# Operand addresses of a TensorE-bound layer moved to 52 bytes apart, with two small moves of work around it

## The chip, the cores and the metric

The kernel runs on one core of a Trainium2 chip, as one program. The metric is the device time of one execution in microseconds. A TensorE matmul is two instructions here: a load of the stationary operand (128 columns), and a matmul that streams the moving operand past it. The load for the next matmul runs beside the current matmul, so both read SBUF at the same time.

## The reference

One decoder layer on x of 512 tokens by 2048 features, all in float32:

```python
xn = rmsnorm(x, norm_w)
proj = xn @ w_in                         # 2048 -> 14352 columns
q, k, v, o, z, i, f, u_g, v_g, z_g = split(proj)
# group A: causal conv + SiLU on q, k; 8 mLSTM heads (chunks of 128, gates from i, f);
#          per-head RMSNorm, then * sigmoid(o) * silu(z)
# group B: gelu(u_g) * (tril(w_spatial) @ layernorm(gelu(v_g)) + b_spatial) * silu(z_g)
y = concat(y_m, y_g)                     # 4096
out = rmsnorm(x + y @ w_out, final_norm_w)
```

## The kernel before

**Products in three passes.** A float32 operand is split into a rounded part (`wh`, `xah`, ...: a cast by ACT to float32r) and a rest (`wl`, `xal`, ...: a subtraction by DVE), and each product is three matmuls: high with high, high with low, low with high.

**Phase A, the input projection**, is 28 units (`unit_order`), each with 8 chunks of the contraction. Unit 0 is computed directly: four PSUM banks `p_0` to `p_3` (one for each 128 tokens), matmuls with 512 moving columns (L760 to L769; the gate columns, L282, run beside it). Units 1 to 27 use a scheme of seven products for a 2x2 block (`PRODUCTS`, the function `products`, L798): a chunk is 7 products x 2 halves x 3 passes = 42 matmuls with 256 moving columns, into seven banks, which `combine` (L371 to L378) adds up on DVE at the unit's end. That is 27 x 8 x 42 = 9,072 matmuls. In a token unit the stationary operand is a slice of x and the moving one a slice of w; in the four `qk` units (features) it is the other way round. A chunk of weights comes by a DMA from SP (L150) with an adding DMA from POOL (L151) on top, and is split by `split` (L183 to L187): `wf` is the raw chunk, `we` two sums made by DVE, `wh` and `wl` the split tiles of 7 x 256 columns.

**Phase B, the output projection**, has 32 chunks of kind `g` (direct, 512 columns, L853 to L855), beside which the mLSTM heads are computed, 24 chunks of kind `m` (seven products again, the same L798: 1,008 matmuls), and a last part in 512 columns (L917 to L919).

**What sets the order.** Everything that follows a unit (activations, norms, transposes, the heads) is put on a queue `bg`, of which the loops take a few items after each chunk (`run_bg(3)` in phase A, `run_bg(6)` in phase B). The code's order is only a priority: when the program is built, a scheduler puts each engine's instructions into one fixed queue, by that priority and by when it takes operands and buffers to be ready. Tiles of one tag share a fixed number of buffers, handed out in the code's order (12 for `temp`).

**At the end of unit 0** ACT reads the four banks with a GELU (L774) into the tiles `e_00` to `e_11`; `bn_stats` on DVE (L411) follows, from `after_vv`. Products q1, q6, q2 and q7 of unit 1 need the banks of `p_0`, `p_1`, `p_2` and `p_3` in that order. **At the end of unit 27** a loop (L815) empties `bg`: the sigmoid and SiLU of the last unit (L496, `after_oz`) come before phase B's own work.

**Where operands lie.** The pools are laid out one after the other, with two gaps (`GAP_X`, `GAP_W`) and an offset inside the direct chunks' tiles (`OFF`). In the built program the start addresses are, in bytes modulo 128: x operands and the seven-product w tiles 0 and 64, so that moving and stationary operands of L798 start 64 apart; operands of the 512-column matmuls 0 and 0, but for the `a21` tiles (`a` in the profile; stationary in a fourth of unit 0's matmuls) at 32.

Of the kernel before, what the change touches and what calls it, by code (L numbers as in the profile page):

```python
# [9 lines left out]
F32 = mybir.dt.float32  # L10
# [22 lines left out]
    ("q1", 0, 1), ("q6", 4, 5), ("q2", 1, 0), ("q7", 3, 4), ("q5", 6, 3), ("q4", 2, 6), ("q3", 5, 2),  # L33
]
WS = 7 * H
OFF = 16
GAP_X, GAP_W = 24, 112


def unit_order():  # L40
# [7 lines left out]
def hybrid_layer(ctx, tc, xs, x, w_first, w_mid, w_gate, w_out, w_last, par, bif, ws_t, sgu, fin_w, out):  # L48
# [17 lines left out]
    def temp(name, dt=F32):  # L66
        return tp.tile([P, S], dt, tag="t", name=name)
# [11 lines left out]
    for w in range(9):  # L79
# [16 lines left out]
    mask = one.tile([P, P], F32, name="mask")
    nc.gpsimd.memset(mask, 0.0)
    nc.gpsimd.affine_select(
        out=mask, in_=mask, pattern=[[1, P]], compare_op=ALU.is_ge,
        fill=BIG, base=0, channel_multiplier=-1,  # L100
    )
# [17 lines left out]
    chunks = []  # L119
    for un in range(NA):  # L120
        for j in range(NP):
            chunks.append(("std", w_first[j]) if un == 0 else ("str", w_mid[un - 1, j]))
    NB0 = len(chunks)
    b_chunks = []
    for kind in "gm":
# [26 lines left out]

    def split_first(a):
        if 0 not in splits:
            splits[0] = tuple(wp.tile([P, WS], F32R, tag=tag, name=f"{tag}0", bufs=3)[:, OFF:OFF + 1024].rearrange(
                "p (a b) -> p a b", a=2) for tag in ("wh", "wl"))
        h, l = splits[0]
        f = raws[0][:, a * S:(a + 1) * S]
        nc.scalar.copy(h[:, a, :], f)
        nc.vector.tensor_tensor(l[:, a, :], f, h[:, a, :].bitcast(F32), op=ALU.subtract)  # L160

    def split(n):
        if n >= NCH or n in splits:
            return
        kind = chunks[n][0]
        t = raws[n]
        raws[n] = None
        if kind == "std":
            if n >= NF0 + 2:
                h = xb.tile([P, 2, S], F32R, tag="xb", name=f"fh{n}")  # L170
                l = xb.tile([P, 2, S], F32R, tag="xb", name=f"fl{n}")
            else:
                h, l = (wp.tile([P, WS], F32R, tag=tag, name=f"{tag}{n}", bufs=bufs)[
                    :, OFF:OFF + 1024].rearrange("p (a b) -> p a b", a=2) for tag, bufs in (("wh", 3), ("wl", 3)))
            f = t[:, 0:1024].rearrange("p (a b) -> p a b", a=2)
            nc.scalar.copy(h, f)  # L176
            nc.vector.tensor_tensor(l, f, h.bitcast(F32), op=ALU.subtract)  # L177
            splits[n] = (h, l)
            return
        h = wp.tile([P, WS], F32R, tag="wh", name=f"wh{n}", bufs=3)  # L180
        l = wp.tile([P, WS], F32R, tag="wl", name=f"wl{n}", bufs=3)
        e = wp.tile([P, 2 * H], F32, tag="we", name=f"we{n}", bufs=1)
        nc.vector.tensor_tensor(e[:, 0:H], t[:, 3 * H:4 * H], t[:, 2 * H:3 * H], op=ALU.add)  # L183
        nc.vector.tensor_tensor(e[:, H:2 * H], e[:, 0:H], t[:, 0:H], op=ALU.add)  # L184
        for f, c in ((t, slice(0, 5 * H)), (e, slice(5 * H, WS))):
            nc.scalar.copy(h[:, c], f)  # L186
            nc.vector.tensor_tensor(l[:, c], f, h[:, c].bitcast(F32), op=ALU.subtract)  # L187
        splits[n] = tuple(v.rearrange("p (a b) -> p a b", a=7) for v in (h, l))
# [58 lines left out]
            nc.scalar.activation(t, t, AF.Square, accum_out=ssq8[:, tt, c:c + 1])  # L247

    def stats_end():
        ssq = sm.tile([P, NT], F32, tag="s4", name="ssq", bufs=8)  # L250
        nc.vector.reduce_sum(ssq, ssq8, axis=mybir.AxisListType.X)
        nc.vector.tensor_scalar(ssq, ssq, 1.0 / D, EPS, op0=ALU.mult, op1=ALU.add)
        nc.gpsimd.tensor_tensor(r_tok, ssq, mhalf[:, :NT], op=ALU.pow)
# [143 lines left out]
    def after_vv(i, c):  # L397
        mv = sm.tile([P, 2, NT, 2], F32, tag="mv", name=f"mv{i}")
        rs = sm.tile([P, 2, NT], F32, tag="rs", name=f"rs{i}")
        nm = sm.tile([P, 2, NT], F32, tag="nm", name=f"nm{i}")  # L400
        for g in range(2):
            vn[2 * i + g] = [c[0][g], c[1][g]]

        def gelu(g, a):
            for t in range(2):
                tt = 2 * a + t
                d = c[a][g][:, t, :]
                if i > 0:
                    nc.scalar.activation(d, d, AF.Gelu_apprx_tanh, scale=r_tok[:, tt:tt + 1])
                st = sm.tile([P, 6], F32, tag="st", name=f"st{i}_{tt}_{g}", bufs=4)  # L410
                nc.vector.bn_stats(st, d)  # L411
                nc.vector.bn_aggr(mv[:, g, tt, :], st)

        def scales():
            vv = sm.tile([P, 2, NT], F32, tag="vv", name=f"vv{i}")
            nc.vector.tensor_scalar(vv, mv[:, :, :, 1], EPS, None, op0=ALU.add)
            nc.gpsimd.tensor_tensor(rs, vv, mhalf.rearrange("p (a b) -> p a b", a=2), op=ALU.pow)
            nc.vector.scalar_tensor_tensor(nm, in0=mv[:, :, :, 0], scalar=-1.0, in1=rs, op0=ALU.mult, op1=ALU.mult)

        def norm(g, a):  # L420
            d = c[a][g]
            for t in range(2):
                tt = 2 * a + t
                nc.scalar.activation(d[:, t, :], d[:, t, :], AF.Identity, scale=rs[:, g, tt:tt + 1],
                                     bias=nm[:, g, tt:tt + 1])
            wb = wb_t[2 * i + g]
            nc.vector.tensor_tensor(d, d, wb[:, 0:1, :].to_broadcast([P, 2, H]), op=ALU.mult)
            nc.vector.tensor_tensor(d, d, wb[:, 1:2, :].to_broadcast([P, 2, H]), op=ALU.add)

        bg.append(lambda: st_ws(i))  # L430
        for g in range(2):
            for a in range(2):
# [112 lines left out]
    def st_load_v(h):  # L545
        for a in range(2):
            t = half(f"vr{h}_{a}")
            nc.gpsimd.dma_start(t, v_dram[h][:, 2 * a:2 * a + 2, :])
            hi, lo = (xa.tile([P, 3 * H], F32R, tag="xa", name=f"v{c}{h}_{a}").rearrange(
                "p (a b) -> p a b", a=2)[:, :, 112:370] for c in "hl")  # L550
            for t2, one_or_zero in ((hi, 1.0), (lo, 0.0)):
                nc.gpsimd.memset(t2[:, :, H:258].bitcast(F32), one_or_zero)
            nc.scalar.copy(hi[:, :, 0:H], t)
            nc.vector.tensor_tensor(lo[:, :, 0:H], t, hi[:, :, 0:H].bitcast(F32), op=ALU.subtract)
            v_t[h].append((hi, lo))
# [5 lines left out]
    def st_s(h, s0):  # L561
# [9 lines left out]
        pt = temp(f"p{h}_{s0}")  # L571
        cb = cb_t[h]
        g = gst[:, pair(s0, s0), h:h + 1]
        nc.vector.scalar_tensor_tensor(pt[:, 0:P], in0=cb[:, s0 * P:(s0 + 1) * P], scalar=g, in1=mask,
                                       op0=ALU.subtract, op1=ALU.max)
        nc.scalar.activation(pt[:, 0:P], pt[:, 0:P], AF.Exp, scale=-1.0)
        for t0 in range(s0 + 1, NT):
# [34 lines left out]
    def st_norm(h):  # L612
# [3 lines left out]
            nc.gpsimd.dma_start(t, oz_dram[h][:, 2 * a:2 * a + 2, :])  # L616
            oz_t[h].append(t)
        ht = h_t[h]
        da = sm.tile([P, NT], F32, tag="s4", name=f"da{h}", bufs=8)
        nc.vector.scalar_tensor_tensor(da, in0=den_t[h], scalar=-1.0, in1=den_t[h], op0=ALU.mult, op1=ALU.max)  # L620
        nc.vector.tensor_tensor(da, da, gst[:, 10:14, h], op=ALU.max)
        rr = sm.tile([P, NT], F32, tag="s4", name=f"rr{h}", bufs=8)
        nc.vector.reciprocal(rr, da)
        ssq = sm.tile([P, NT], F32, tag="s4", name=f"sq{h}", bufs=8)
        junk = temp(f"jk{h}")[:, 0:H]
        for t0 in range(NT):
            nc.scalar.activation(junk, ht[t0 // 2][:, t0 % 2, 0:H], AF.Square, scale=rr[:, t0:t0 + 1],
                                 accum_out=ssq[:, t0:t0 + 1])
        nc.vector.tensor_scalar(ssq, ssq, 1.0 / H, EPS, op0=ALU.mult, op1=ALU.add)
        rn = sm.tile([P, NT], F32, tag="s4", name=f"rn{h}", bufs=8)  # L630
        nc.gpsimd.tensor_tensor(rn, ssq, mhalf[:, :NT], op=ALU.pow)
        hc = sm.tile([P, NT], F32, tag="hc", name=f"hc{h}", bufs=4)
        nc.vector.tensor_tensor(hc, rr, rn, op=ALU.mult)
# [78 lines left out]
    def run_bg(k):  # L712
        while k > 0 and bg:
            bg.popleft()()
            k -= 1
# [2 lines left out]
        while tag not in done:  # L718
            bg.popleft()()

    act_warm = sm.tile([P, 8], F32, tag="aw", name="act_warm", bufs=1)
    nc.scalar.copy(act_warm, mhalf)

    load_x(0)
# [46 lines left out]
    c0 = [[half(f"e0_{a}{g}") for g in range(2)] for a in range(2)]  # L771
    for q in range(4):
        for g in range(2):
            nc.scalar.activation(c0[q // 2][g][:, q % 2, :], acc[q][:, g * H:(g + 1) * H], AF.Gelu_apprx_tanh,  # L774
                                 scale=r_tok[:, q:q + 1])
# [25 lines left out]
    for un in range(1, NA):  # L801
        kind, i = order[un]
        q = product_banks(un)
        for j in range(NP):
# [7 lines left out]
            if un == NA - 1 and j >= 1:  # L812
                load_y("g", j - 1)
            run_bg(3)
    while bg:  # L815
        run_bg(1)
    load_y("g", NP - 1)
    bg.append(gates)
    queue_loads(0)
    bg.extend([pause] * 6)  # L820
    bg.append(gate_shifts)
# [200 lines left out]
```

## Time and profile before

| | us |
|---|---|
| median of 3 runs (1563.46, 1564.47, 1569.3) | 1564.47 |
| the profiled execution, its own time | 1571.57 |
| span of the profiled execution | 1569.9 |
| TensorE (PE) matmul busy / load busy (PEld) | 1545.9 / 1485.4 |
| DVE busy / ACT busy / POOL busy | 1183.7 / 874.6 / 285.3 |

A busy PE says only that some matmul is under way: a matmul of 256 columns is recorded as 0.28 us long, while the next starts some 0.12 us after it, so that two or three overlap. How fast PE goes is read from the starts: from a pair of rows of the timeline, or from how many matmuls fall into a stretch of given length.

### The profile page before, as it was taken

What the parts mean: (1) busy time and instruction counts of PE and PEld (TensorE: products, weight loads), DVE (VectorE), ACT (ScalarE), POOL (GpSimd) and SP (SyncE); (2) the same over time, 40 slices, a digit from 0 to 9 for tenths busy, and PEclk for the clock granted to TensorE, in tenths of its full rate; (3) what the DMA queues carried; (4) which work ended last, traced back from release to release, by engine and by line L of the source; (5) the groups of instructions that cost most, each with busy time, mean ns of one, the idle gap of its engine ahead of it and who ended that gap; (6) DMA issues with size and microseconds to landing.
All of it is one profiled execution on the core that took longest, in us unless ns stands there. A gap on an engine that the chain in (4) does not pass through costs nothing. (4 is left out here: it accounts for less than half of the span.)

```text
span 1569.9 us, 30095 instructions
## 1 busy us (share of the span) xinstructions
PE 1545.9 (98%) x11864; PEld 1485.4 (95%) x11864; DVE 1183.7 (75%) x1944; ACT 874.6 (56%) x1340; POOL 285.3 (18%) x384
## 2 busy tenths in 40 slices
PE   9999999999999999999999999999999999999997
PEld 7899999999999999999999999999988788889986
DVE  8787767877966876976877977678887665697875
ACT  6665455654654555554655565454776666553333
POOL 1411112211122211121211111111202222011100
PEclk9999999999999999999999999999999999999999
DMA  9777878787788777778787777877964665798962
GB/s 319 210 192 187 228 177 209 185 202 193 213 203 215 188 211 184 210 190 214 192 211 186 200 203 199 212 201 196 277 195 156 206 226 188 238 265 238 277 231 107
DMA packets 118510, 326.99 MB, mean 208 GB/s; under 512 B 13534, under 2 KB 20702, under 8 KB 118369
## 3 DMA queue, kind: packets, MB, share of 16 engines
q1 hardware_dynamic: 77456, 243.30, 48.1%
q0 software_dynamic: 40192, 80.66, 26.7%
q8 instruction: 93, 1.52, 0.4%
q10 hardware_dynamic: 720, 1.11, 0.2%
q14 instruction: 49, 0.39, 0.1%
HBM read 229.37 MB, written 32.74 MB: 167 GB/s over the span
## 5 line engine op out<-in xcount | busy, mean ns | idle before, releaser
L186 ACT CAST wh<-wf 128x1280 fp32r<-128x1280 f32 x240 | 301.9, 1264 | 379.9 <-issue 237.8
L187 DVE TENSOR_TENSOR wl<-wf,wh 128x1280 fp32r<-128x1280 f32 x240 | 356.7, 1488 | 174.3 <-ACT wh L186 174.0
L798 PE MATMUL q<-wh,xbh 128*128 128x256 f32 x1472 | 413.7, 281 | 1.4 <-ACT e L774 1.4
L798 PE MATMUL q<-wl,xbh 128*128 128x256 f32 x1472 | 412.9, 281 | 1.2 <-DVE wl L187 1.2
L798 PE MATMUL q<-wh,xbl 128*128 128x256 f32 x1472 | 412.7, 280 | 0.0
L151 POOL DMA_DIRECT2D wf<-wf x240 | 205.3, 857 | 1010.9 <-DMA wf<-w_mid 243.2
L798 PE MATMUL q<-wh,xah 128*128 128x256 f32 x1104 | 311.8, 282 | 0.0
L798 PE MATMUL q<-wl,xah 128*128 128x256 f32 x1104 | 309.5, 280 | 0.0
L798 PE MATMUL q<-wh,xal 128*128 128x256 f32 x1104 | 309.4, 280 | 0.0
L798 PEld LDWEIGHTS q<-wh,xbh 128*128 128x128 f32 x1472 | 281.1, 191 | 1.8 <-ACT e L774 1.6
L798 PEld LDWEIGHTS q<-wl,xbh 128*128 128x128 f32 x1472 | 276.9, 188 | 1.9 <-DVE wl L187 1.8
L798 PEld LDWEIGHTS q<-wh,xbl 128*128 128x128 f32 x1472 | 276.3, 188 | 0.0
L798 PEld LDWEIGHTS q<-wh,xah 128*128 128x128 f32 x1104 | 210.8, 191 | 0.7 <-ACT e L774 0.2
L798 PEld LDWEIGHTS q<-wl,xah 128*128 128x128 f32 x1104 | 207.7, 188 | 0.1
L798 PEld LDWEIGHTS q<-wh,xal 128*128 128x128 f32 x1104 | 207.2, 188 | 0.0
L186 ACT CAST wh<-we 128x512 fp32r<-128x512 f32 x240 | 148.2, 618 | 89.6 <-DVE we L184 89.2
L187 DVE TENSOR_TENSOR wl<-we,wh 128x512 fp32r<-128x512 f32 x240 | 164.7, 686 | 17.2 <-ACT wh L186 17.2
L183 DVE TENSOR_TENSOR we<-wf 128x256 f32<-128x256 f32 x240 | 101.4, 422 | 20.0 <-issue 9.0
L184 DVE TENSOR_TENSOR we<-we,wf 128x256 f32<-128x256 f32 x240 | 101.4, 423 | 5.4
L853 PE MATMUL og<-wh,ygh 128*128 128x512 f32 x256 | 100.9, 396 | 1.6 <-ACT wh L176 1.6
L854 PE MATMUL og<-wl,ygh 128*128 128x512 f32 x256 | 101.5, 397 | 0.1
L855 PE MATMUL og<-wh,ygl 128*128 128x512 f32 x256 | 101.3, 396 | 0.0
(284 smaller groups left out, 2865.9 us busy)
## 6 DMA issues: line engine op xcount, KB each, us to landing
wf<-w_mid SPq DMA_DIRECT2D x216, 640.0 KB, 4.7
wf<-wf POOLq DMA_DIRECT2D x240, 256.0 KB, 5.2
wf<-w_out_p SPq DMA_DIRECT2D x40, 512.0 KB, 4.1
wf<-w_last SPq DMA_DIRECT2D x24, 640.0 KB, 5.7
xr<-xs SPq DMA_DIRECT2D x16, 256.0 KB, 6.1
xt<-x SPq DMA_DIRECT2D x8, 512.0 KB, 7.5
ozd<-e SPq DMA_DIRECT2D x16, 256.0 KB, 2.6
ygd<-yfg SPq DMA_DIRECT2D x16, 256.0 KB, 4.5
```

The lines of the kernel that those rows point to most:

```text
L151: nc.gpsimd.dma_start(t[:, 3 * H:5 * H], t[:, H:3 * H], accum_op=ALU.add)
L183: nc.vector.tensor_tensor(e[:, 0:H], t[:, 3 * H:4 * H], t[:, 2 * H:3 * H], op=ALU.add)
L184: nc.vector.tensor_tensor(e[:, H:2 * H], e[:, 0:H], t[:, 0:H], op=ALU.add)
L186: nc.scalar.copy(h[:, c], f)
L187: nc.vector.tensor_tensor(l[:, c], f, h[:, c].bitcast(F32), op=ALU.subtract)
L798: nc.tensor.matmul(o, lhsT=st_, rhs=mv_, start=(first and a == 0), stop=(last and a == 2), skip_group_check=True)
L853: nc.tensor.matmul(acc[q], lhsT=yh[:, kk, cs], rhs=wh[:, kk, :], start=st, stop=False)
L854: nc.tensor.matmul(acc[q], lhsT=yh[:, kk, cs], rhs=wl[:, kk, :], start=False, stop=False)
L855: nc.tensor.matmul(acc[q], lhsT=yl[:, kk, cs], rhs=wh[:, kk, :], start=False, stop=sp_)
```

## The change

It does three things.

1. The split tiles of the seven-product chunks start at other places. Their slots grow by 64 columns (`WSLOT`), and a chunk lies 3 columns into it (`OFF_TOK`) for a token unit and for phase B, 29 columns (`OFF_FEAT`) for a `qk` unit; the gaps shrink, and the v operands of the heads move from column 112 to 115. In the built program the moving operand of L798 then starts at 76 and the stationary one at 0 modulo 128 bytes (`qk` units: 0 and 52): the stationary operand is 52 bytes beyond the moving one in both. The 512-column operands stay at 0 and 0, `a21` goes from 32 to 64. To make room, `mask` and `act_warm` become `temp` tiles (the mask is made by POOL after phase A) and the tag `s4` has 6 buffers in place of 8.
2. At the end of unit 0 the banks are emptied as scaled copies, `p_0` and `p_2` by ACT, `p_1` and `p_3` by DVE; the GELU runs afterwards, in SBUF, as an item of `bg`.
3. The loop that empties `bg` before phase B is gone: what is left of unit 27 is taken by phase B's `run_bg(6)`.

```diff
-OFF = 16
-GAP_X, GAP_W = 24, 112
+WSLOT = WS + 64
+OFF, OFF_TOK, OFF_FEAT = 16, 3, 29
+GAP_X, GAP_W = 16, 48
...
-            chunks.append(("std", w_first[j]) if un == 0 else ("str", w_mid[un - 1, j]))
+            chunks.append(("std", w_first[j]) if un == 0 else
+                          ("strf" if order[un][0] == "qk" else "str", w_mid[un - 1, j]))
...
-        h = wp.tile([P, WS], F32R, tag="wh", name=f"wh{n}", bufs=3)
-        l = wp.tile([P, WS], F32R, tag="wl", name=f"wl{n}", bufs=3)
+        o = OFF_FEAT if kind == "strf" else OFF_TOK
+        h, l = (wp.tile([P, WSLOT], F32R, tag=tag, name=f"{tag}{n}", bufs=3)[:, o:o + WS] for tag in ("wh", "wl"))
...
-                if i > 0:
-                    nc.scalar.activation(d, d, AF.Gelu_apprx_tanh, scale=r_tok[:, tt:tt + 1])
+                nc.scalar.activation(d, d, AF.Gelu_apprx_tanh, scale=r_tok[:, tt:tt + 1] if i > 0 else 1.0)
...
-                "p (a b) -> p a b", a=2)[:, :, 112:370] for c in "hl")
+                "p (a b) -> p a b", a=2)[:, :, 115:373] for c in "hl")
...
-    act_warm = sm.tile([P, 8], F32, tag="aw", name="act_warm", bufs=1)
+    act_warm = temp("act_warm")[:, 0:8]
...
-            nc.scalar.activation(c0[q // 2][g][:, q % 2, :], acc[q][:, g * H:(g + 1) * H], AF.Gelu_apprx_tanh,
-                                 scale=r_tok[:, q:q + 1])
+            d, ps = c0[q // 2][g][:, q % 2, :], acc[q][:, g * H:(g + 1) * H]
+            if q % 2:
+                nc.vector.tensor_scalar(d, ps, r_tok[:, q:q + 1], None, op0=ALU.mult)
+            else:
+                nc.scalar.activation(d, ps, AF.Copy, scale=r_tok[:, q:q + 1])
...
-    while bg:
-        run_bg(1)
     load_y("g", NP - 1)
     bg.append(gates)
+    bg.append(make_mask)
```

The scheduler moves instructions with it, at three places. First, the start. `act_warm` is a scratch copy that waits for a memset on POOL; `a_0` is the high part of the `a21` tile. ACT before:

```order
L217 CAST xah_186<-xr_172 128x256
L218 CAST a_0_188<-xr_172 128x256
L159 CAST wh_193<-wf_174 128x512 x2
L223 CAST xah_186<-xr_172 128x512
L217 CAST xah_208<-xr_178 128x256
L218 CAST a_1_210<-xr_178 128x256
L722 COPY act_warm<-mhalf 128x8
```

ACT with the change, at the same place:

```order
L224 CAST xah_181<-xr_167 128x256
L166 CAST wh_188<-wf_169 128x512 x2
L230 CAST xah_181<-xr_167 128x512
L224 CAST xah_203<-xr_173 128x256
L230 CAST xah_203<-xr_173 128x512
L728 COPY act_warm<-mhalf 128x8
L225 CAST a_0_183<-xr_167 128x256
```

`a_0` now comes after `act_warm`, whose tile is handed out before it; PE does the twelve matmuls of `p_0` and `p_1` first and those of `p_2` and `p_3`, which need `a_0`, after them. Second, the end of unit 0. DVE with the change (`e_..` are the copies, `st` and `mv` the statistics, `we` and `wl` the next chunk's split):

```order
L417 BN_STATS st_0_0_829<-e_00_734 128x6
L190 TENSOR_TENSOR we_675<-wf_609 128x256
L782 TENSOR_SCALAR e_00_734<-p_1_218,r_tok 128x256
L191 TENSOR_TENSOR we_675<-we_675,wf_609 128x256
L782 TENSOR_SCALAR e_01_735<-p_1_218,r_tok 128x256
L418 BN_AGGR mv_749<-st_0_0_829 128x2
L417 BN_STATS st_1_0_833<-e_00_734 128x6
L418 BN_AGGR mv_749<-st_1_0_833 128x2
L417 BN_STATS st_2_0_891<-e_10_736 128x6
L782 TENSOR_SCALAR e_10_736<-p_3_220,r_tok 128x256
```

DVE's copies of `p_1` and `p_3` stand behind statistics that read ACT's GELU of `p_0` and of `p_2`. On ACT, the table load and the first GELUs stand between the copies of `p_0` and `p_2`:

```order
L784 ACTIVATE e_00_734<-p_0_217,r_tok 128x256
L784 ACTIVATE e_01_735<-p_0_217,r_tok 128x256
L415 ACT_TABLE_LOAD
L415 ACTIVATE e_00_734<-e_00_734 128x256
L415 ACTIVATE e_01_735<-e_01_735 128x256
L415 ACTIVATE e_00_734<-e_00_734 128x256
L784 ACTIVATE e_10_736<-p_2_219,r_tok 128x256
L784 ACTIVATE e_11_737<-p_2_219,r_tok 128x256
L415 ACTIVATE e_10_736<-e_10_736 128x256
L415 ACTIVATE e_01_735<-e_01_735 128x256
L415 ACTIVATE e_11_737<-e_11_737 128x256
L193 CAST wh_673<-wf_609 128x1280
```

Before, ACT alone emptied them, the table load first:

```order
L774 ACT_TABLE_LOAD
L774 ACTIVATE e_00_739<-p_0_222,r_tok 128x256
L774 ACTIVATE e_01_740<-p_0_222,r_tok 128x256
L774 ACTIVATE e_00_739<-p_1_223,r_tok 128x256
L774 ACTIVATE e_01_740<-p_1_223,r_tok 128x256
L774 ACTIVATE e_10_741<-p_2_224,r_tok 128x256
L774 ACTIVATE e_11_742<-p_2_224,r_tok 128x256
L186 CAST wh_678<-wf_614 128x1280
L186 CAST wh_678<-we_680 128x512
L774 ACTIVATE e_10_741<-p_3_225,r_tok 128x256
L774 ACTIVATE e_11_742<-p_3_225,r_tok 128x256
```

With the change ACT has eight GELUs more and four copies fewer there, and the split `wh` of unit 1's second chunk stands behind ten activations and the table load, where it stood behind six and the table load. Third, the seam between the phases (`e_0` to `e_3` are unit 27's results, `ygh` the loaded group-B outputs, `wh` the third chunk of phase B). ACT before:

```order
L496 ACT_TABLE_LOAD
L496 ACTIVATE e_0_13784<-e_0_13784,r_tok 128x256 x2
L496 ACT_TABLE_LOAD
L496 ACTIVATE e_1_13785<-e_1_13785,r_tok 128x256
L677 CAST ygh_13796<-yrg_0_13798 128x512
L677 CAST ygh_13796<-yrg_1_13802 128x512
L496 ACT_TABLE_LOAD
L496 ACTIVATE e_3_13787<-e_3_13787,r_tok 128x256 x2
L496 ACT_TABLE_LOAD
L496 ACTIVATE e_2_13786<-e_2_13786,r_tok 128x256 x2
L496 ACTIVATE e_1_13785<-e_1_13785,r_tok 128x256
```

After one more pair of `ygh` casts follows `CAST wh_13830`. With the change:

```order
L502 ACT_TABLE_LOAD
L502 ACTIVATE e_0_13787<-e_0_13787,r_tok 128x256 x2
L183 CAST wh_13827<-wf_13681 128x1024
L683 CAST ygh_13799<-yrg_0_13801 128x512
L683 CAST ygh_13799<-yrg_1_13805 128x512
L502 ACTIVATE e_3_13790<-e_3_13790,r_tok 128x256 x2
L502 ACT_TABLE_LOAD
L502 ACTIVATE e_2_13789<-e_2_13789,r_tok 128x256 x2
```

The cast of `wh` comes after the first pair of activations, and there are two table loads where there were four. In phase B itself the heads' matmuls are dealt out among the `og` matmuls in another order than before, of the same count.

More of the change, by code (lines that the diff above doesn't have):

```diff
@@ L95, in hybrid_layer, with make_mask @@
     nc.gpsimd.memset(mhalf, -0.5)
[L96 to L101, printed above, removed]
+    masks = []
+    def make_mask():
+        mask = temp("mask")[:, 0:P]
+        nc.gpsimd.memset(mask, 0.0)
+        nc.gpsimd.affine_select(
+            out=mask, in_=mask, pattern=[[1, P]], compare_op=ALU.is_ge,
+            fill=BIG, base=0, channel_multiplier=-1,
+        )
+        masks.append(mask)
     r_tok = one.tile([P, NT], F32, name="r_tok")
@@ L154, in split_first @@
         if 0 not in splits:
-            splits[0] = tuple(wp.tile([P, WS], F32R, tag=tag, name=f"{tag}0", bufs=3)[:, OFF:OFF + 1024].rearrange(
+            splits[0] = tuple(wp.tile([P, WSLOT], F32R, tag=tag, name=f"{tag}0", bufs=3)[:, OFF:OFF + 1024].rearrange(
                 "p (a b) -> p a b", a=2) for tag in ("wh", "wl"))
@@ L172, in split @@
             else:
-                h, l = (wp.tile([P, WS], F32R, tag=tag, name=f"{tag}{n}", bufs=bufs)[
+                h, l = (wp.tile([P, WSLOT], F32R, tag=tag, name=f"{tag}{n}", bufs=bufs)[
                     :, OFF:OFF + 1024].rearrange("p (a b) -> p a b", a=2) for tag, bufs in (("wh", 3), ("wl", 3)))
@@ L249, in stats_end @@
     def stats_end():
-        ssq = sm.tile([P, NT], F32, tag="s4", name="ssq", bufs=8)
+        ssq = sm.tile([P, NT], F32, tag="s4", name="ssq", bufs=6)
         nc.vector.reduce_sum(ssq, ssq8, axis=mybir.AxisListType.X)
@@ L573, in st_s @@
         g = gst[:, pair(s0, s0), h:h + 1]
-        nc.vector.scalar_tensor_tensor(pt[:, 0:P], in0=cb[:, s0 * P:(s0 + 1) * P], scalar=g, in1=mask,
+        nc.vector.scalar_tensor_tensor(pt[:, 0:P], in0=cb[:, s0 * P:(s0 + 1) * P], scalar=g, in1=masks[0],
                                        op0=ALU.subtract, op1=ALU.max)
@@ L618, in st_norm @@
         ht = h_t[h]
-        da = sm.tile([P, NT], F32, tag="s4", name=f"da{h}", bufs=8)
+        da = sm.tile([P, NT], F32, tag="s4", name=f"da{h}", bufs=6)
         nc.vector.scalar_tensor_tensor(da, in0=den_t[h], scalar=-1.0, in1=den_t[h], op0=ALU.mult, op1=ALU.max)
         nc.vector.tensor_tensor(da, da, gst[:, 10:14, h], op=ALU.max)
-        rr = sm.tile([P, NT], F32, tag="s4", name=f"rr{h}", bufs=8)
+        rr = sm.tile([P, NT], F32, tag="s4", name=f"rr{h}", bufs=6)
         nc.vector.reciprocal(rr, da)
-        ssq = sm.tile([P, NT], F32, tag="s4", name=f"sq{h}", bufs=8)
+        ssq = sm.tile([P, NT], F32, tag="s4", name=f"sq{h}", bufs=6)
         junk = temp(f"jk{h}")[:, 0:H]
@@ L629, in st_norm @@
         nc.vector.tensor_scalar(ssq, ssq, 1.0 / H, EPS, op0=ALU.mult, op1=ALU.add)
-        rn = sm.tile([P, NT], F32, tag="s4", name=f"rn{h}", bufs=8)
+        rn = sm.tile([P, NT], F32, tag="s4", name=f"rn{h}", bufs=6)
         nc.gpsimd.tensor_tensor(rn, ssq, mhalf[:, :NT], op=ALU.pow)
```

## Prediction

> **What bounds the kernel now.** First the page: its first line, the busy times, and the group that repeats most.
>
> ```profile
> span 1569.9 us, 30095 instructions
> PE 1545.9 (98%) x11864; PEld 1485.4 (95%) x11864; DVE 1183.7 (75%) x1944; ACT 874.6 (56%) x1340; POOL 285.3 (18%) x384
> L798 PE MATMUL q<-wh,xbh 128*128 128x256 f32 x1472 | 413.7, 281 | 1.4 <-ACT e L774 1.4
> ```
>
> PE never rests and next to nothing releases it late: behind 1,472 matmuls stand 1.4 us of waiting. So the time is the number of matmuls times the distance between two starts, which the 281 ns of one do not tell. The busy time by stretch, of L798 alone, gives it. The columns are the stretch, its length, PE's and PEld's busy time with counts, the granted clock, DMA share and GB/s.
>
> ```profile
> 60.00:1152.00 1092.00, 1074.68 (x9065) 1067.18 (x9066) 1.00 0.78 203
> 1395.00:1516.00 121.00, 119.11 (x1008) 118.72 (x1007) 1.00 0.92 267
> ...
> 410.00:436.00 26.00, 26.00 (x232) 26.00 (x231) 1.00 0.81 216
> 510.00:536.00 26.00, 26.00 (x224) 26.00 (x222) 1.00 0.66 165
> ```
>
> L798 owns 1,213 of the 1,570 us with some 10,075 matmuls. The lower two rows are the find: two stretches of 26 us without a gap, the clock 1.00 in both, the same form of instruction, and one holds 232 matmuls, the other 224. Some three of each count began before the stretch (each is recorded 0.28 us long), so 229 and 221 starts: 113.5 and 117.6 ns. I call them the fast and the slow pace. The fast pace is rare; these rows are all of its stretches longer than 5 us, with the breaks by transposes inside them:
>
> ```profile
> 154.02:161.00 6.98, 6.27 (x51) 5.78 (x49) 1.00 0.53 144
> 235.76:242.90 7.14, 6.43 (x52) 5.89 (x50) 1.00 0.64 172
> 388.75:444.80 56.05, 54.64 (x473) 53.85 (x471) 1.00 0.74 196
> 680.83:687.90 7.07, 6.36 (x52) 5.89 (x50) 1.00 0.70 173
> 923.85:930.90 7.05, 6.34 (x52) 5.89 (x50) 1.00 0.62 156
> 1073.86:1113.50 39.64, 39.45 (x348) 39.25 (x346) 1.00 0.78 208
> 1144.50:1150.00 5.50, 5.50 (x51) 5.50 (x50) 1.00 0.43 144
> ```
>
> That is 1,079 matmuls; some 9,000 go at the slow pace. A pace starts and ends at a break (a wait, a transpose between the products) and then holds for hundreds of matmuls. The operands' addresses are 64 bytes apart in both, so this distance admits both paces and the trace does not say which one another distance selects. That an address matters at all is seen in unit 0's 512-column matmuls. Those on the `a` tiles load a stationary operand that starts at 32 modulo 128; those of the output projection have all operands at 0.
>
> ```profile
> 17.36 0.39 PE L767 MATMUL p<-wh,a 128*128 128x512 f32 x1
> ...
> 18.06 0.40 PE L767 MATMUL p<-wh,xah 128*128 128x512 f32 x1
> ...
> 1159.01 0.39 PE L853 MATMUL og<-wh,ygh 128*128 128x512 f32 x1
> ...
> 1160.37 0.39 PE L853 MATMUL og<-wh,ygh 128*128 128x512 f32 x1
> ```
>
> Three starts in 0.70 us with `a`, 233 ns each; six in 1.36 us at 0, 227 ns. An operand moved by 32 bytes thus goes with 6 to 7 ns a matmul, at a place where nothing waits.
>
> **The change, part by part.** *The distance* (9,072 + 1,008 L798 matmuls). The trace has no matmul at 52, so it is bounded. Downward by the fast pace: 9,000 x (117.6 - 113.5 = 4.1 ns) = 37 us less. Upward by the `a` rows: 10,080 x 6.6 ns = 66 us more. I take the fast end. The nearest rows are those of L798 itself, which show that these matmuls can go at 113.5 ns, and nothing in between: 227 ns for 512 columns is twice 113.5, so the 256-column matmul at the fast pace loses nothing to the load beside it, and the slow pace is 4.1 ns lost to that load. [...] The 240 matmuls of the heads' values (258 columns) get the same distance: 1 us at the same 4.1 ns.
>
> [...]
>
> *The shifted writes.* ACT and DVE now write `wh` and `wl` 12 bytes off. The nearest row that writes off a boundary (4, 8 or 12 bytes) is L520, which also has a third operand:
>
> ```profile
> L520 DVE SCALAR_TENSOR_TENSOR qc<-qs,prm,qc 128x511 f32<-128x511 f32 x16 | 11.9, 746 | 0.0
> L187 DVE TENSOR_TENSOR wl<-we,wh 128x512 fp32r<-128x512 f32 x240 | 164.7, 686 | 17.2 <-ACT wh L186 17.2
> 873.04:912.60 39.56, 39.56 (x338) 39.56 (x337) 36.95 (x60) 21.92 (x26) 6.68 (x8) 1.00 0.80 211
> ```
>
> So 0 to 60 ns per 512 columns, or 0 to 0.2 us a chunk. It is hidden by DVE's idle quarter. The last row (all engines: PE, PEld, DVE, ACT, POOL) is one of the units in which DVE is fullest: 36.95 of 39.56 us. At the fast pace the unit takes 38.1, and 8 x 0.2 us would fill it to 38.6: at worst half a microsecond in such a unit, if the three raw chunks in hand did not cover it. I take 0.
>
> *Unit 0's banks.* Now the products of unit 1 wait for the last bank, and the GELUs on ACT set that:
>
> ```profile
> 58.08 1.28 ACT L774 ACT_TABLE_LOAD   x1
> 59.37 2.30 ACT L774 ACTIVATE e<-p,r_tok 128x256 f32<-128x256 f32 x6
> 61.53 1.29 ACT L186 CAST wh<-wf 128x1280 fp32r<-128x1280 f32 x1
> 62.68 0.66 ACT L186 CAST wh<-we 128x512 fp32r<-128x512 f32 x1
> 63.20 0.88 ACT L774 ACTIVATE e<-p,r_tok 128x256 f32<-128x256 f32 x2
> 62.42 0.28 PE L798 MATMUL q<-wh,xal 128*128 128x256 f32 x1
> 64.13 0.39 PE L798 MATMUL q<-wh,xbh 128*128 128x256 f32 x1 [1.43 <-ACT e L774]
> ```
>
> q7 starts at 64.13, 1.6 us after it could. The new queues keep a chain through both engines. From 58.05, when ACT comes free: two copies (0.38 each), table load 1.28, GELU 0.5: 60.6. Then DVE's statistics 0.4 and a `we` 0.34 (both at their rows' usual length, an estimate), and its two copies of `p_1` around another `we`, at 0.4: `p_1` is free at 62.5, q6 waits for it from 60.7 on, and 1.8 us are lost there. ACT's third GELU needs the first of these copies; copies of `p_2`, GELU, DVE's third statistics and the copies of `p_3` follow: 64.4 against 64.1. The wait moves from the fourth product to the second and keeps its size: 0, between -1.6 (all banks in time) and +2 (DVE's statistics each wait for ACT a little longer, and `wh` of the next chunk with them).
>
> *The seam.* The third chunk of phase B waited for its `wh`:
>
> ```profile
> 1153.62 1.28 ACT L496 ACT_TABLE_LOAD   x1
> ...
> 1163.42 1.12 ACT L677 CAST ygh<-yrg 128x512 fp32r<-128x512 f32 x2
> 1164.45 1.04 ACT L176 CAST wh<-wf 128x1024 fp32r<-128x1024 f32 x1
> ...
> 1163.50:1165.50 2.00, 0.43 (x2) 0.01 (x1) 2.00 (x4) 1.99 (x4) 1.31 (x6) 1.00 0.36 133
> 1165.50:1170.20 4.70, 4.56 (x12) 3.37 (x13) 3.98 (x6) 3.80 (x4) 0.00 (x0) 0.64 0.87 268
> ```
>
> PE loses 1.8 us of the first stretch, and after the gap its clock is granted at 0.64 over 4.70 us: 1.7 us more. The cast now stands thirteen instructions earlier, ahead of what were three table loads: -3.5 us, between -3.5 and 0. Late next is the fourth `wh`, behind some 8 us of ACT work (four `ygh`, six activations, two table loads, the logarithm), which is two chunks' time at most (24 matmuls of 0.227 us are 5.4); the chunk split ahead covers it.
>
> *The start.* `a_0` moves behind `act_warm`:
>
> ```profile
> 5.69 0.40 ACT L218 CAST a<-xr 128x256 fp32r<-128x256 f32 x1
> 10.97 0.19 ACT L722 COPY act_warm<-mhalf 128x8 f32<-128x8 f32 x1
> 13.66 0.40 PE L767 MATMUL p<-wh,xah 128*128 128x512 f32 x1
> ```
>
> `act_warm` at 11.2 (the cast of 512 columns is now ahead of it), `a_0` until 11.7, its low part on DVE until 12.1, then ten of the twelve matmuls of `p_2` and `p_3` at 0.23: 14.5 in place of 13.66. +0.9 us, between 0 and +2.
>
> *Phase B's heads* are dealt out anew. Their waits now are
>
> ```profile
> PE ytm L473 <- DVE oz L639: 2.5, 1, 2.5
> PE ytm L473 <- DVE p L580: 1.3, 3, 0.6
> ```
>
> and each may grow or go: -4 to +4, taken as 0. The mask takes one of 12 `temp` buffers there, and POOL has two instructions of a fraction of a microsecond more, both inside this range; SP's queue trades places of neighbours only. In unit 0 one weight load goes behind two loads of x, three chunks ahead of its use: 0. Six `s4` buffers for four tiles a head: 0.
>
> **Sum.** -37 - 1 - 3.5 + 0.9 = -41 us on the execution of 1571.6 us: 1531. The median of the runs is 1564.5, 7 us less than that execution. If the plain runs have a larger share of the fast pace, they gain less and end at 1531 too; if not, at 1524. I take 1527.
>
> **The rivals.** *Nothing moves the pace*: the fast pace comes of the breaks, as it does at 64, and the distance has no say. For it: one distance, two paces. Then -3.5 + 0.9 remains: 1562, within 0.5% (7.8 us, about what a measurement of this kernel can tell from no change). *A part goes fast*: each break throws the pace back, and the 20 or so units' transposes do it in mid-unit. Half the gain: 1544. [...]
> [...]
>
> **How the numbers follow.** Fast nearly everywhere: 57%, 1512 to 1542 (the two ends above, -4 and +4 of phase B, a tenth of the matmuls still slow). A part fast: 9%, to 1557. Below 1512: 2%. No change of pace: 16%, 1557 to 1572. Worse: 16%, above 1572, most of it near 1580. Faster 0.68, same 0.16, slower 0.16. For 8 in 10 the range needs the fast case, the partial one and most of the unchanged: 1512 to 1568.
>
> **What would show it.** In the profile after: 26 us in mid-unit hold 232 matmuls of L798's successor everywhere, also after transposes; PEld and PE stay without gaps. The first products of unit 1 wait for a DVE copy, by 1 to 2 us. No wait for `wh` at the third chunk of phase B, and no clock below 1 behind it. The start ends a microsecond later. I am wrong if the counts stay at 224, or fall.

## The result: 1.4% slower, and the profile after

The median of the changed kernel is 1584.26 us (1580.59 to 1585.1) against 1563.97 for the kernel before: ratio 1.0144, 95% interval 1.01 to 1.0188. The forecast was 1527. The profiled execution took 1584.11 us, 12.5 more than the profiled one of before; the other 7.6 us are that this execution of before was itself slow for its kernel. First the page of the changed kernel; L807 is what was L798.

```profile
span 1582.2 us, 30121 instructions
PE 1552.3 (98%) x11864; PEld 1492.1 (94%) x11864; DVE 1186.6 (75%) x1948; ACT 873.6 (55%) x1342; POOL 281.8 (18%) x384
L807 PE MATMUL q<-wh,xbh 128*128 128x256 f32 x1472 | 413.2, 281 | 2.1 <-DVE mv L418 2.1
L807 PE MATMUL q<-wl,xbh 128*128 128x256 f32 x1472 | 413.6, 281 | 0.0
```

Nothing there tells the loss: PE is as full as before and waits as little. The pace does. Busy time by stretch, of L807 alone, in the middle of a token unit, of another, of phase B's products and of a `qk` unit:

```profile
408.00:434.00 26.00, 26.00 (x219) 26.00 (x218) 1.00 0.83 227
480.00:506.00 26.00, 26.00 (x224) 26.00 (x222) 1.00 0.85 222
1412.00:1438.00 26.00, 26.00 (x225) 26.00 (x224) 1.00 0.88 244
1046.00:1072.00 26.00, 26.00 (x232) 26.00 (x231) 1.00 0.82 224
```

Four paces, and only the `qk` unit has the fast one. From the starts in the trace they are 120.0, 117.8, 116.7 and 113.3 ns. Some 3,200 of the 10,080 products go at 120.0, a pace that the kernel before did not have; the token unit behind each `qk` unit is one of them. I call the sum of the distances from each of phase A's 9,072 products to the next start "products of phase A": 1078.5 us, 1074.9 before.

The second loss is between unit 27 and the first m chunk. All engines, before and then after:

```profile
1152.80:1394.90 242.10, 235.57 (x1186) 197.66 (x1184) 163.12 (x342) 151.76 (x370) 45.35 (x101) 0.99 0.66 212
```

```profile
1159.20:1408.00 248.80, 238.55 (x1186) 199.91 (x1185) 161.79 (x340) 149.97 (x367) 45.25 (x103) 0.97 0.64 206
```

6.7 us more for the same matmuls. The seam itself did what was forecast: in its stretch PE is busy throughout (13.00 of 13.00 us) at clock 1.00.

```profile
1159.00:1172.00 13.00, 13.00 (x61) 10.80 (x59) 11.30 (x19) 12.62 (x20) 2.98 (x10) 1.00 0.98 306
```

The loss is in the heads. The waits of PE, and one place in time order (transposes of a head, three products of its values, then four `og` matmuls):

```profile
PE ytm L479 <- DVE p L586: 3.4, 5, 1.4
...
PE nv L612 <- DVE p L586: 2.3, 2, 1.2
PE ytm L479 <- DVE oz L645: 2.2, 3, 0.9
PE q L807 <- DVE mv L418: 2.1, 2, 1.8
PE rb_ps L267 <- DVE diag L266: 1.7, 1, 1.7
```

```profile
1234.81 1.12 PE L479 MATMUL ytm<-ident,oz 128*128 128x128 f32 x8 [1.40 <-DVE p L586]
1237.09 0.36 PE L612 MATMUL nv<-vh,sh 128*128 128x258 f32 x1 [1.15 <-DVE p L586]
...
1237.67 0.63 PE L861 MATMUL og<-wh,ygh 128*128 128x512 f32 x1
1238.10 0.63 PE L862 MATMUL og<-wl,ygh 128*128 128x512 f32 x1
```

Ten of the heads' waits for DVE stand there where the prediction's rows had four. Behind the longer ones the `og` matmuls start 0.43 us apart instead of 0.23, for some 3 us at half the granted clock (third number from the right). The stretch has four such pieces, each of which loses 1.7 us:

```profile
1237.50:1240.70 3.20, 3.20 (x10) 2.52 (x10) 2.36 (x5) 2.72 (x8) 0.83 (x6) 0.50 0.81 292
1281.70:1285.10 3.40, 3.40 (x11) 2.82 (x11) 3.24 (x8) 3.09 (x8) 0.96 (x6) 0.50 0.54 130
1309.00:1312.40 3.40, 3.40 (x10) 2.70 (x9) 2.37 (x5) 2.73 (x8) 0.85 (x6) 0.50 0.84 276
1353.40:1356.80 3.40, 3.40 (x10) 2.64 (x9) 3.23 (x7) 2.23 (x7) 1.15 (x2) 0.50 0.41 101
```

The last two rows of the waits above are unit 1's. DVE, at the time of the last one (`diag` is what `rb_ps` waits for):

```profile
68.08 0.28 DVE L266 TENSOR_SCALAR diag<-ident,r_tok 128x128 f32<-128x128 f32 x1
...
68.62 1.49 DVE L194 TENSOR_TENSOR wl<-wf,wh 128x1280 fp32r<-128x1280 f32 x1
...
70.35 0.67 DVE L266 TENSOR_SCALAR diag<-ident,r_tok 128x128 f32<-128x128 f32 x3
```

Three of the four `diag` stand behind the split of a chunk.

### The profile page after: what moved, and what is told of

The parts are those of the page before. It is cut to its first block, busy times and chain, and to the rows that moved or that the text cites. A ratio compares the mean times of both kernels' runs of the same rounds, so it can differ in the third digit from the quotient of the medians.

```text
span 1582.2 us, 30121 instructions
## 1 busy us (share of the span) xinstructions
PE 1552.3 (98%) x11864; PEld 1492.1 (94%) x11864; DVE 1186.6 (75%) x1948; ACT 873.6 (55%) x1342; POOL 281.8 (18%) x384
## 5 line engine op out<-in xcount | busy, mean ns | idle before, releaser
L807 PE MATMUL q<-wh,xbh 128*128 128x256 f32 x1472 | 413.2, 281 | 2.1 <-DVE mv L418 2.1
L807 PE MATMUL q<-wl,xbh 128*128 128x256 f32 x1472 | 413.6, 281 | 0.0
L807 PE MATMUL q<-wh,xbl 128*128 128x256 f32 x1472 | 412.1, 280 | 0.0
L807 PE MATMUL q<-wh,xah 128*128 128x256 f32 x1104 | 311.1, 282 | 0.0
L807 PE MATMUL q<-wl,xah 128*128 128x256 f32 x1104 | 310.2, 281 | 0.0
L807 PE MATMUL q<-wh,xal 128*128 128x256 f32 x1104 | 309.1, 280 | 0.0
L807 PEld LDWEIGHTS q<-wh,xbh 128*128 128x128 f32 x1472 | 277.9, 189 | 2.6 <-issue 2.4
L807 PEld LDWEIGHTS q<-wh,xbl 128*128 128x128 f32 x1472 | 280.1, 190 | 0.0
L807 PEld LDWEIGHTS q<-wl,xbh 128*128 128x128 f32 x1472 | 277.9, 189 | 0.1
L807 PEld LDWEIGHTS q<-wh,xal 128*128 128x128 f32 x1104 | 210.0, 190 | 0.0
L807 PEld LDWEIGHTS q<-wl,xah 128*128 128x128 f32 x1104 | 208.4, 189 | 0.1
L807 PEld LDWEIGHTS q<-wh,xah 128*128 128x128 f32 x1104 | 208.4, 189 | 0.1
```

The lines of the kernel that those rows point to most:

```text
L807: nc.tensor.matmul(o, lhsT=st_, rhs=mv_, start=(first and a == 0), stop=(last and a == 2), skip_group_check=True)
```

## Experiments

Each run is compared with the kernel before, measured beside it on the same chip; times are medians.

**1 to 3. Each edit alone**, in the kernel before. The first (slots of 32 spare columns are enough for both offsets, so `mask`, `act_warm` and `s4` stay where they were; the rest of the edit is as in the change):

```diff
-OFF = 16
-GAP_X, GAP_W = 24, 112
+WSLOT = WS + 32
+OFF, OFF_TOK, OFF_FEAT = 16, 3, 29
+GAP_X, GAP_W = 24, 48
...
```

> The kernel before with the first edit alone (operands of L798's successor 52 bytes apart; mask, act_warm, s4, unit 0 and the loop before phase B as before). Theory A (the distance is one cause among three; it makes the qk units fast and throws the token unit behind each of them to 120.0 ns): products of phase A 1074 to 1080 us, the qk units at 113.3 ns, units 9, 15, 21, 26 at 120.0, phase B's heads as before; profiled execution 1571 to 1577, the median 1564 to 1577. Theory B (the distance carries the whole loss, through phase B too): profiled 1582 to 1586. Theory C (the prediction's: all at the fast pace, and something else in the change lost it): 1530 to 1545.

1563.33 us, ratio 1.0002 (0.9988 to 1.0015). Theories B and C fall, and A in its main number: the token units went at 116.6 and 117.8 ns, none at 120.0. (With slots of 32 only 55% of the token units' products are at the change's distance; 7 and 8 say why.)

```profile
395.00:421.00 26.00, 26.00 (x225) 26.00 (x223) 1.00 0.86 219
1040.00:1060.00 20.00, 20.00 (x179) 20.00 (x178) 1.00 0.87 230
```

The `qk` units are fast here too (second row: some 177 starts in 20 us, 113 ns). Products of phase A: 1068.2 us.

The second: the copies at the end of unit 0 and `scale=... if i > 0 else 1.0`, as in the change.

> The kernel before with the second edit alone (banks of unit 0 emptied by DVE and ACT as scaled copies, GELU later). Theory A: q6 waits about 1.9 us for DVE, q7 no longer 1.6, and the matmul of token_rows (rb_ps) waits about 1.9 us for DVE: unit 1 ends some 2.3 us later, the rest unchanged; profiled 1572 to 1576. Rival (that wait came of the changed start or the shifted writes): unit 1 ends within 0.5 us of before.

1564.81 us, ratio 1.0006 (0.9989 to 1.0023). PE's waits in unit 1:

```profile
61.45 0.36 PE L800 MATMUL q<-wh,xbh 128*128 128x256 f32 x1 [0.69 <-DVE e L775]
63.78 0.36 PE L800 MATMUL q<-wh,xbh 128*128 128x256 f32 x1 [0.67 <-DVE mv L411]
68.50 0.94 PE L260 MATMUL rb_ps<-diag,ones 128*128 128x128 f32 x6 [1.51 <-DVE diag L259]
```

The waits for the banks are 1.4 us, where the whole change has 2.1 and theory A had 1.9 for q6 alone. The one at rb_ps is there without the other edits, so the rival falls. The profiled execution, 1560.85 us, is far under A's 1572 to 1576, and its products tell why: some 4,400 of 10,080 at the fast pace and products of phase A at 1063.9 us, with the operands 64 bytes apart as before, whose profiled execution had some 1,060.

The third:

```diff
-    while bg:
-        run_bg(1)
     load_y("g", NP - 1)
```

> The kernel before with the third edit alone (the loop that empties the background queue before phase B removed). Theory A (this edit deals the heads out so that their transposes and products wait): from the last product of unit 27 to the first of the m chunks 248 to 249 us against 242.1 before: the seam 5 us less, waits of ytm, tps and nv 10 to 12 us more; profiled 1576 to 1580. Rival (the mask in one of the 12 temp buffers, or six s4 buffers, makes the heads wait): 237 to 240 us between these two, profiled 1566 to 1569.

1558.87 us, ratio 0.9971 (0.9955 to 0.9988): this edit alone is a gain, and theory A falls. From unit 27 to the m chunks:

```profile
1144.20:1380.60 236.40, 230.72 (x1185) 195.52 (x1184) 164.57 (x343) 148.44 (x368) 44.94 (x101) 1.00 0.67 219
```

236.4 against 242.1, where the whole change has 248.8. Here too many products were fast (some 3,840; 1065.5 us in phase A). So none of the three edits loses anything alone; unless they act on one another, what the whole loses lies in what came with them, the slots of 64 and the tiles moved to make room for them.

**4. A sweep of the distance.** The changed kernel with an offset of its own for each pair of chunks:

```diff
+SWEEP = [
+    [4, 12, 24, 2],
...
-        o = OFF_FEAT if kind == "strf" else OFF_TOK
+        o = SWEEP[n // NP - 1][n % NP // 2] if n < NB0 else OFF_TOK
```

> The changed kernel, but each pair of chunks of units 1 to 27 has an offset of its own: the moving operand of the token units stands at each multiple of 4 modulo 128 three times (stationary at 0), the stationary one of the qk units at each multiple of 8 once (moving at 0). Theory A (the address selects among a few paces and a break or a change of address moves the state): the mean spacing of a pair takes the values 113.3, 116.7, 117.8 and 120.0 ns and few others; the same offset gives the same set of values in its three places; some offsets give 113.3 in all three. [...] Rival (the address has no say): 117.8 nearly everywhere with changes at breaks only, whatever the offset.

1587.11 us in one run. The distance is that of the moving operand beyond the stationary one; two pairs at 4 and two at 28:

```profile
200.50:208.50 8.00, 8.00 (x67) 8.00 (x67) 1.00 0.78 204
988.80:996.80 8.00, 8.00 (x67) 8.00 (x66) 1.00 0.89 225
415.00:423.00 8.00, 8.00 (x71) 8.00 (x71) 1.00 0.84 243
926.50:934.50 8.00, 8.00 (x71) 8.00 (x71) 1.00 0.76 194
```

Hundreds of us apart, the same distance gives the same count: 123.3 and 115.5 ns. Theory A holds but for two points: the values are more than a few (some dozen, from 113.3 to 123.3), and no distance of this half is at 113.3 in all its places. Address does select the pace.

**5, 6. The slots and the mask.** The changed kernel with `WSLOT = WS + 32`:

> The changed kernel with slots of 32 in place of 64 spare columns for the split tiles (the first operand of a chunk at the same address modulo 128, the three buffers 128 apart modulo 256 in place of equal). Each of the three edits alone cost nothing (ratios 1.000, 1.001, 0.997), so what the whole change loses is in none of them. Theory A (two things beside the edits lose it: the slots' pitch, which throws token units to 120.0 ns where the distance alone gave 116.6 and 117.8; and the mask in a temp buffer, which deals phase B's heads out so that they wait): products of phase A 1067 to 1070 us against 1078, from unit 27 to the m chunks still 248 to 250; profiled 1571 to 1575. Rival B (120.0 ns comes of x lying 640 bytes lower, or of the breaks): products 1077 to 1080, profiled 1581 to 1586.

1570.26 us, ratio 1.0068 (1.0044 to 1.0093); products of phase A 1066.0 against 1078.5, with no unit at 120.0. The two programs have the same instructions in the same order on every engine; only addresses differ. These are the same places in the program as above:

```profile
408.00:434.00 26.00, 26.00 (x225) 26.00 (x223) 1.00 0.81 224
480.00:506.00 26.00, 26.00 (x225) 26.00 (x224) 1.00 0.79 200
```

The rest, 242.6 us from unit 27 to the m chunks, missed A's 248 to 250, and so the profiled 1566.66 us its 1571 to 1575. The waits are the same but a little shorter (the pair shown above is 0.68 and 1.15 us here, not 1.40 and 1.15), and the clock stays at 1.00 behind them:

```profile
1224.10:1227.30 3.20, 3.20 (x16) 2.65 (x17) 2.35 (x5) 2.65 (x9) 1.10 (x6) 1.00 0.78 264
```

So the changed kernel's four pieces at half the clock (6.8 us) are about the whole difference of 6.2 us in this stretch, and the order of the work alone does not bring them.

The same with the mask as it was before the change:

> The same, with the mask back in a place of its own, made at the start, so that the heads have 12 temp buffers (act_warm in a temp buffer and six s4 buffers stay). Theory A: from unit 27 to the m chunks 235 to 239 us as with the seam alone (236.3), products of phase A as in f1_slot32; profiled 1558 to 1563, the ratio 0.996 to 1.001. Rival C (six s4 buffers or act_warm, not the mask): 247 to 250 us there, profiled 1571 to 1575.

1563.84 us, ratio 1.0031 (1.0003 to 1.0059); 237.5 us from unit 27 to the m chunks. Experiment 5, then this one:

```profile
1147.20:1389.80 242.60, 234.41 (x1185) 195.00 (x1184) 162.18 (x340) 150.72 (x366) 45.35 (x103) 1.00 0.65 212
1148.20:1385.70 237.50, 232.14 (x1186) 194.69 (x1184) 164.61 (x343) 148.45 (x368) 44.88 (x101) 1.00 0.67 217
```

The stretch is as theory A had it, the ratio a little over its 0.996 to 1.001. But the reason given for it (the temp buffer) was not tested by it, since with the mask also its item on the queue went.

**7, 8. The best offsets of the sweep** in the kernel of experiment 1, with the loop removed too (here 28; for 108 the middle number is 11):

```diff
-OFF, OFF_TOK, OFF_FEAT = 16, 3, 29
+OFF, OFF_TOK, OFF_FEAT = 16, 23, 29
```

> The kernel before with the loop before phase B removed, and the split tiles so that the moving operand of the token units stands at 28 modulo 128 (stationary 0), and the stationary one of the qk units at 52 (moving 0); slots of 32 spare columns. In the sweep 28 gave 115.5 ns in its three places, 52 in the qk units 113.3. Theory A (address alone, whatever the slots' pitch): token units 115.5 from break to break, products of phase A 1055 to 1058 us against 1065 with the seam alone, 240 less 4 from unit 27 to the m chunks; profiled 1542 to 1548, ratio 0.986 to 0.990. Rival (the pitch of the slots changes the pace of each offset): two or three paces in turn over the three buffers, 117 to 119 in the mean, profiled 1556 to 1568.

> The same with the moving operand of the token units at 108 modulo 128, which gave 115.6 ns in its three places of the sweep. Theory A: as h1_at28, profiled 1542 to 1548. Rival: the pitch decides; paces in turn over the three buffers and 1556 to 1568.

1560.59 and 1563.6 us, ratios 0.999 (0.9963 to 1.0017) and 1.0015 (0.999 to 1.0039). The rival was right: the three buffers take turns, at 115.6, 117.7 and 117.1 ns with 28, at 115.5, 119.7 and 116.8 with 108. Three chunks of the latter one after the other:

```profile
104.20:109.00 4.80, 4.80 (x43) 4.80 (x43) 1.00 0.87 201
109.20:114.00 4.80, 4.80 (x44) 4.80 (x43) 1.00 0.85 217
114.20:118.90 4.70, 4.70 (x41) 4.70 (x41) 1.00 0.80 204
```

With slots of 32 the buffers lie 128 bytes apart modulo 256, so two distances alternate, for `wh` and `wl` each. In the built program of experiment 7 one of the three buffers has both parts 28 bytes beyond the stationary operand modulo 256 (115.6 ns), one has both at 156 (117.7), and one has `wh` at 28 and `wl` at 156 (117.1). Where the sweep's buffers differed by 256 bytes, one distance had one pace (but for those with several).

This also tells the distance from the moving operand's own address. The stationary operand starts at 128 modulo 256 here and at 0 in the sweeps. The buffer at 115.6 ns has its moving operand at 156, an address that goes at 117.8 in the second sweep (10, below), where it is a distance of 156. So it is the distance that counts.

**9. The item of the queue.** The changed kernel, with its slots of 64 and its mask in a temp buffer:

```diff
-    bg.append(make_mask)
+    make_mask()
```

> The changed kernel (slots of 64, mask in a temp buffer) with the mask made by a plain call before phase B in place of an item of the background queue, of which phase B takes six after each chunk. Theory A (the one item more shifts which work of the heads is issued beside which chunk, and so makes the heads wait): from unit 27 to the m chunks 236 to 240 us against 248.7, products of phase A 1077 to 1080 as in the changed kernel; profiled 1570 to 1576. Rival (one temp buffer less makes the heads wait): 246 to 250, profiled 1581 to 1586.

1578.24 us, ratio 1.008 (1.0045 to 1.0115), 6 us under the changed kernel as they stand (10 by the ratios), and

```profile
1162.00:1400.50 238.50, 231.30 (x1185) 195.91 (x1183) 164.10 (x343) 151.51 (x368) 44.52 (x101) 0.99 0.66 216
```

10 us less than with the item. Some 5 of them are the clock: one piece at half the clock here, four in the changed kernel. The other 5 are what experiments 5 and 6, both at a clock of 1.00, have between them. So the item costs some 5 us by itself, and the buffer next to nothing (238.5 us with the mask in it, 237.5 without). Theory A is right on this stretch and a little off beside it: products of phase A 1081.5 us, profiled 1578.24. Its reason is read from the code, not measured: phase B takes six items after each chunk, and one item more near the head of the queue puts each piece of the heads one place later among the chunks.

**10. The sweep's other half** (the same edit, offsets 32 to 63):

> The sweep over the other half of 256 bytes (each offset 128 bytes further than in e4_sweep). Theory A (the pace depends on the distance modulo 256, as the three buffers of h1_at28 and h2_at108 suggest): offsets whose values differ from those 128 bytes lower: the distance 156 (28 and 128) 117 to 118 ns where 28 gave 115.5, 108 120 ns where 236 gave 115.6, 76 always 116.7 where 204 gave three paces; each offset repeats in its three places. Rival (modulo 128 alone): the same values as in e4_sweep, offset by offset.

1596.28 us in one run. At 156 117.8 ns where 28 gave 115.5, at 108 120.0 where 236 gave 115.5, at 76 116.7 where 204 has three paces: modulo 256 it is. And one distance is fast in all its three places, 112 (first three rows; the last two are 84):

```profile
117.00:125.00 8.00, 8.00 (x73) 8.00 (x72) 1.00 0.82 232
509.50:517.50 8.00, 8.00 (x72) 8.00 (x71) 1.00 0.79 179
1153.50:1161.50 8.00, 8.00 (x73) 8.00 (x72) 1.00 0.68 166
499.50:507.50 8.00, 8.00 (x68) 8.00 (x67) 1.00 0.78 184
283.50:291.50 8.00, 8.00 (x67) 8.00 (x67) 1.00 0.73 151
```

Token units, 64 distances, mean ns of each of the places (worked out from the starts, without the first dozen products of a place and without breaks):

| distance mod 256 | ns | distance mod 256 | ns |
|---|---|---|---|
| 112 | 113.3, 113.5, 113.3 | 204 (the change) | 117.6, 117.8, 117.8 |
| 192 (before) | 113.3, 114.4, 117.8 | 108 | 120.0, 120.0, 120.0 |
| 144 | 113.3, 118.6, 118.7 | 116 | 121.7, 121.7, 121.7 |
| 28 and 236 | 115.5 to 115.6 in all six | 20; 84 | 122.2; 122.8, each in all three |
| 12, 60, 76, 140 | 116.7 in all twelve | 4 | 123.3, 123.3, 123.3 |

One place stands outside: 104 went at 130.0 in one place (123 and 137 ns in turn) and at 120.0 in its other two.

**11, 12. The distance of 112.** One number of the changed kernel:

```diff
-OFF, OFF_TOK, OFF_FEAT = 16, 3, 29
+OFF, OFF_TOK, OFF_FEAT = 16, 44, 29
```

> The changed kernel with one number altered: OFF_TOK 44 in place of 3, so that the moving operand of the token units lies 112 bytes beyond the stationary one modulo 256 (204 in the changed kernel), for the high and the low parts and in all three buffers alike. In the sweep 112 gave 113.3 to 114 ns in its three places, where all but three other distances gave 115.5 and more. Theory A (the distance modulo 256 sets the pace, the prediction had only taken the wrong one): every token unit at 113.3 also behind transposes, products of phase A 1039 to 1044 us against 1078, of the m chunks 116 to 118; the rest as in the changed kernel; profiled 1540 to 1548, ratio to before 0.985 to 0.991. Rival (the state is set at breaks, and the sweep's three places were luck): products 1060 to 1078, profiled 1565 to 1584.

1550.67 us, ratio 0.9925 (0.9905 to 0.9945): 33.6 us less than the changed kernel, by one number, with the same instructions in the same order on every engine. Between the profiled executions the products of phase A are 29.6 us of it; most of the rest is the stretch from unit 27 to the m chunks, 242.8 us as in experiment 5, whose operands the number doesn't touch. More than 9,000 of the 10,080 products are fast, behind transposes too:

```profile
464.00:490.00 26.00, 26.00 (x232) 26.00 (x231) 1.00 0.89 228
1013.00:1039.00 26.00, 26.00 (x232) 26.00 (x231) 1.00 0.76 206
```

And with it the seam's edit, unit 0 and `act_warm` as before the change, and the mask, made by a plain call as in 9, in the buffer of phase A's `ws`, which is free by then:

```diff
-        mask = temp("mask")[:, 0:P]
+        mask = sm.tile([P, 2, P], F32, tag="ws", name="mask", bufs=1)[:, 0, :]
...
```

> The distance of 112, the loop before phase B removed, unit 0 and act_warm as before, the mask in the buffer that phase A's ws tiles leave (made by a plain call). Theory A: products of phase A 1039 to 1044 us, from unit 27 to the m chunks 235 to 239, no wait at rb_ps; profiled 1524 to 1532, ratio 0.974 to 0.980. Rival as above: 1550 to 1560.

1541.3 us, ratio 0.9871 (0.9848 to 0.9894), the fastest of all. Both gain less than was expected of them: products of phase A 1048.9 and 1049.8 us, not 1039 to 1044. The waits of PE in the last kernel show the rest:

```profile
PE q L805 <- DVE wl L194: 4.4, 9, 1.2
...
PE q L805 <- DVE e L380: 1.4, 1, 1.4
```

In nine places DVE's split is now late; the changed kernel's group of the `wl` products above has 0.0 us of waiting. The longest of these waits is followed by a piece at half the clock, 1.7 us more:

```profile
1117.00:1120.40 3.40, 3.40 (x19) 3.40 (x18) 3.40 (x7) 1.14 (x2) 0.00 (x0) 0.51 0.28 76
```

That is some 7 us together. The plain runs of this kernel (1540 to 1544) are some 7 us over its profiled one (1534.7); why is open.

## Why the prediction was wrong

**The distance** (-37 us) is the step that failed. In its place the products of phase A took 3.6 us more (1078.5 against 1074.9). That these matmuls can go at 113.5 ns and that an address decides over it was right, and the size nearly so: with 112 bytes the same products take 26.0 us less than in the profiled execution of before, and 29.6 less than in the changed kernel. What failed is "I take the fast end": that the fast pace exists at one distance was taken as a reason to expect it at another. The change's distance, 204 modulo 256, has three paces of its own in the token units (116.7, 117.8 and 120.0 ns), none of them the fast one. The bounds held it, the choice between them had no row, and 64 distances show that it had poor odds: one is always fast, two are at times. To lie near the fast distance was worth nothing: 108 and 116 lie next to 112 and go at 120.0 and 121.7. That the slow pace is 4.1 ns lost to the load beside the matmul was my reading; no run tells the load's share. Why one distance is fast and the next is not stays open. "They are 64 apart in both" was also too coarse: the pace repeats with the distance modulo 256, and I gave the addresses modulo 128.

The chances had a slower pace at 16%, most of it near 1580. The result, 1584.26 us, lies close to that, but no run shows the term behind this figure; in its place the products of phase A took 3.6 us more, and the rest came from elsewhere (below). The sweeps do have a slower side: where the distance is a multiple of 16 bytes, the mean of all pairs is 117.8 ns and the best 113.3; at the other distances they are 119.6 and 115.5, and none of these, the change's among them, had the fast pace in the token units. That is a mean and no more: 28, which is no multiple of 16, goes at 115.5 and beats 14 of the 16 that are, and the `qk` units of the changed kernel, whose stationary operand starts at 52 and whose moving one at 0, were at 113.3. Against the rival by which nothing moves the pace the runs decide: the pace follows the distance of the two operands, and one number took 29.6 us off the products of phase A.

**The gain was partly there already.** The one trace of before had some 1,060 fast products; those of experiments 3 and 2, which keep its distance, had some 3,840 and 4,400, and 9 to 11 us less in the products of phase A. That is likely why the median of before lies 7.6 us under its profiled execution, which the prediction allowed for only as far as it left the end at 1531.

**What the change needed for room** was costed at nothing. The slots of 64 make the three buffers alike modulo 256, all at 204, where those of 32 had `wh` and `wl` partly at 76, and they put many token units at 120.0: 8 us (experiments 9 and 6 by their ratios, 1.0080 and 1.0031) to 12 (the whole change and experiment 5, 1.0144 and 1.0068). The mask's item cost some 5 us, and 10 in the profiled execution, in which the clock fell behind its waits. Both together are the loss: without either the changed kernel is 0.3% (0.03 to 0.59) over before.

**Phase B's heads** (0, from -4 to +4): they lost 12 us against the seam's edit alone (248.8 against 236.4), 6.8 of them by the clock. That the heads were dealt out anew was seen in the order; that one item more on the queue could do it, and that the clock could double it, was not asked.

**Unit 0's banks** (0, with q6 waiting 1.8 us): q6 and q7 together waited 2.1 us for DVE, as said. Not foreseen is rb_ps, 1.7 us behind a `wl` of 1.49 us. Before, the two places waited 1.4 and 0.2 us, so this is some +2, the end of the range given.

**The seam** (-3.5) gave 5.7 alone between profiled executions, 4.5 by the ratio (0.9971). **The start** (+0.9) can't be told: the first product of unit 1 starts at 61.06 us, before at 60.27, but experiments 2 and 3, which don't touch the start, have 59.90 and 61.10. **The shifted writes** cost nothing: the `wl` products waited 0.0 us.

## What to carry to other kernels

When a busy engine shows two paces, don't argue which address is the fast one: give each stretch of one run an address of its own and read all of them from one trace, then keep all buffers of the ring alike at the one that stayed fast in every place (112 here, 113.3 to 113.5 ns). Count what an edit needs for room (a tile's pitch, a moved constant, one more item in a queue that is served by count) as edits of their own. Compare more than one execution before a pace seen in one trace is taken for the kernel's.

## What the hardware showed that was not expected

- The distance from one 256-column matmul to the next takes a set of values from 113.3 to 123.3 ns (130.0 in one place), by the distance of moving and stationary operand modulo 256 bytes, at clock 1.00 and with no wait: 4 bytes can make 6.7 ns (108: 120.0; 112: 113.3). 48 of the 64 distances repeated within 0.4 ns in all their places.
- Some distances hold two or three paces (192: 113.3 and 117.8; 204: 116.7, 117.8 and 120.0) and change between them at breaks. What selects one is open; at 192 the number of fast products was some 1,060, 3,840 and 4,400 in one execution each of three kernels.
- The roles are not alike: at 204 modulo 256 the `qk` units (stationary weights) were at 113.3 through most of each of the changed kernel's, the token units never; in experiment 9 all four `qk` units began at 120.0, and one stayed there.
- Waits of 1.40 and 1.15 us close together were followed by 3 us at a granted clock of 0.50; the same two waits at 0.68 and 1.15 us, in the same order of work, by a clock of 1.00.
